# RMSNorm on one core: the first eight rows loaded as four transfers over interleaved partitions

## Chip, core and metric

The kernel runs on one core of a Trainium2 chip. The metric is the device time of one execution in microseconds, taken as the median over runs.

## What is computed

Every row of 512 numbers is divided by its root mean square and multiplied by `gamma`; there are 16 x 1024 = 16,384 rows in float32.

```
def reference(x, gamma):          # x: 16 x 1024 x 512, gamma: 512
    eps = 1e-5
    rms = np.sqrt(np.mean(x ** 2, axis=-1, keepdims=True) + eps)
    return (x / rms * gamma).astype(np.float32)
```

Input and output have 33.55 MB each, and there is little arithmetic per byte.

## The kernel before

The 16,384 rows are cut into four tiles of 128 partitions x 32 rows; a partition's 32 rows of a tile lie side by side in memory (64 KB). Three buffers in SBUF, `slots[0]` to `slots[2]`, hold one whole tile each; tile 3 uses slot 0 again. Each tile is worked on in groups of rows, nine groups in all: tile 0 as rows 0 to 6, 7 to 15 and 16 to 31, the other tiles in halves of 16 rows.

For a group, ScalarE (ACT) squares the rows (L96), VectorE (DVE) sums the squares (L97), ACT takes the root (L102) and DVE the reciprocal (L103). Then the rows are shared out. GpSimd (POOL) takes the last `share` rows and multiplies them by the reciprocal (L109) and by `gamma_b` (L110). The other rows are scaled by ACT, one instruction a row (L118), and multiplied by gamma by DVE in one instruction (L122), which reads gamma from PSUM. Gamma gets to all partitions by a matmul of a column of ones with `gamma_row` (L66); ACT copies it to `gamma_b` (L165) for POOL.

The order of the instructions is written out by hand (`manual_schedule`). All transfers are issued by SyncE (SP), by the helpers `load` (L45) and `store` (L49); SP works through them in the order of the program. At the start the order is: row 0 of tile 0, rows 1 to 7, gamma in five pieces (L58), rows 8 to 15, rows 16 to 31, and half of tile 1:

```
    load(0, 0, 0, 1)
    load(0, 0, 1, 8)
    for c0, c1 in zip(pieces, pieces[1:]):
        nc.sync.dma_start(out=gamma_row[:, c0:c1], in_=gamma.unsqueeze(0)[:, c0:c1])
    load(0, 0, 8, 16)
    load(0, 0, 16, 32)
    load(1, 1, 0, 16)
```

The semaphores of the transfers go round in a ring of eight: the ninth transfer waits until the first has landed, the tenth for the second, and so on. In the trace, the ninth, `load(0, 0, 16, 32)`, waits on the semaphore of the first, and the tenth, `load(1, 1, 0, 16)`, on that of the second.

All further loads and stores are listed in `transfers`, called once per group after DVE's multiplication. The list `before_scale` holds the transfers and POOL instructions that touched the rows of a slot; `times_gamma` uses it to tell the scheduler which earlier accesses need no wait of DVE's own.

Of the kernel before, what the change touches and what calls it, by code (L numbers as in the profile page):

```python
# [9 lines left out]
def kernel(  # L10
# [6 lines left out]
    nc = tc.nc  # L17
# [8 lines left out]
    N, D = xf.shape  # L26
# [3 lines left out]
    xv = xf.rearrange("(t p r) d -> t p r d", p=P, r=R)  # L30
# [9 lines left out]
    slots = [const.tile([P, R, D], fp32, name=f"slot{i}") for i in range(3)]  # L40

    before_scale = []

    def load(t, slot, r0, r1):
        dma = nc.sync.dma_start(out=slots[slot][:, r0:r1], in_=xv[t][:, r0:r1])  # L45
        before_scale.append((slot, r0, r1, dma))
# [3 lines left out]
        before_scale.append((slot, r0, r1, dma))  # L50

    gamma_row = const.tile([1, D], fp32)
    pieces = (0, 128, 224, 320, 416, D)

    load(0, 0, 0, 1)
    load(0, 0, 1, 8)
    for c0, c1 in zip(pieces, pieces[1:]):
        nc.sync.dma_start(out=gamma_row[:, c0:c1], in_=gamma.unsqueeze(0)[:, c0:c1])  # L58
    load(0, 0, 8, 16)
# [106 lines left out]
    for k, group in enumerate(groups):  # L166
        t, g, n, pieces, share = group
# [45 lines left out]
```

## Time and profile before

| | |
|---|---|
| median of 3 runs | 161.58 us (161.57 to 161.68) |
| span of the profiled execution, the time it gives for itself | 160.2 us |
| DVE busy | 112.0 us (70%) |
| ACT busy | 107.8 us (67%) |
| POOL busy | 106.4 us (66%) |
| PE busy | 2.0 us (1%) |
| moved by DMA | 67.12 MB, mean 419 GB/s over the span |
| first instruction of DVE's last multiplication (L122) | 132.05 us, 7.09 us long |

The span is the time from the first to the last instruction of the program; the runs are timed around it and are 1.4 us longer. Busy times of different engines overlap. In the lines below, L45 means line 45 of the kernel file; `A <- B` after a count names what an engine waited for; "slot<-in_x_dram" is a transfer from the input to a slot. A window's line gives its limits in us, its length, the busy time of PE, PE's weight loads, DVE, ACT and POOL with the number of instructions in brackets, the granted TensorE clock, the mean busy share of the 16 DMA engines, and the rate in GB/s.

### The profile page before, as it was taken

How to read it: one execution, taken by the hardware profiler on the slowest of the kernel's cores; microseconds unless marked ns; L12 is line 12 of the kernel's file. 1: busy time of each engine (PE TensorE's matmuls, PEld its weight loads, DVE VectorE, ACT ScalarE, POOL GpSimd, SP SyncE). 2: the span in 40 equal slices, each digit the busy share in tenths (PEclk: the TensorE clock that was granted, in tenths of full speed). 3: DMA queues.
4: the chain of work that ended last, by engine and by line, in shares of the span. 5: the costliest groups of instructions: out<-in, count | busy, mean ns of one | idle time of the engine just before them, and what ended most of it. 6: DMA issues, size and time to landing. Idle time of an engine off the chain costs nothing.

```text
span 160.2 us, 276 instructions
## 1 busy us (share of the span) xinstructions
PE 2.0 (1%) x2; PEld 0.5 (0%) x2; DVE 112.0 (70%) x39; ACT 107.8 (67%) x108; POOL 106.4 (66%) x24
## 2 busy tenths in 40 slices
PE   0050000000000000000000000000000000000000
PEld 0010000000000000000000000000000000000000
DVE  0018098899798999999999999999999009700000
ACT  3071967976999998999899899989960990000000
POOL 1000951994999599999999999999999980000000
DMA  5999999899999899999999999996996996999994
GB/s 189 431 421 475 442 401 458 340 446 491 417 435 494 388 379 383 426 450 475 434 401 426 483 401 393 524 491 295 524 491 295 524 491 295 401 491 417 401 450 196
DMA packets 2747, 67.12 MB, mean 419 GB/s; under 512 B 313, under 2 KB 314, under 8 KB 826
## 3 DMA queue, kind: packets, MB, share of 16 engines
q1 hardware_dynamic: 2746, 67.11, 98.1%
q14 instruction: 1, 0.01, 0.0%
HBM read 33.56 MB, written 33.55 MB: 419 GB/s over the span
## 4 chain that ended last, share of the span: by engine, by line
DVE 59%; ACT 22%; DMA 4%; ACTq 0%; issue 0%; SPq 0%
DVE ss L97 36%; DVE slot L122 23%; ACT slot L118 8%; ACT slot L96 7%; ACT sq_psum L96 6%; DMA slot<-in_x_dram 4%; DVE ss L103 1%; ACT ss L102 1%; ACTq L208 0%; ACT gamma_b L165 0%; SPq L45 0%; ACTq L96 0%
## 5 line engine op out<-in xcount | busy, mean ns | idle before, releaser
L109 POOL TENSOR_TENSOR slot<-slot,ss 128x3584 f32<-128x3584 f32 (+2 forms) x9 | 47.0, 5218 | 24.1 <-DVE ss L103 24.1
L110 POOL TENSOR_TENSOR slot<-slot,gamma_b 128x3584 f32<-128x3584 f32 (+2 forms) x9 | 59.3, 6587 | 0.7
L97 DVE TENSOR_REDUCE ss<-sq_psum 128x7 f32<-128x3584 f32 (+1 forms) x13 | 42.2, 3247 | 13.7 <-ACT sq_psum L96 13.7
L118 ACT ACTIVATE slot<-slot,ss 128x512 f32<-128x512 f32 x75 | 47.3, 706 | 4.7 <-DVE ss L103 4.7
L122 DVE TENSOR_TENSOR slot<-slot,gamma_psum 128x4608 f32<-128x4608 f32 (+2 forms) x9 | 41.3, 4590 | 8.7 <-ACT slot L118 8.7
L96 ACT ACTIVATE sq_psum<-slot 128x3584 f32<-128x3584 f32 (+1 forms) x13 | 34.6, 2658 | 6.4 <-DMA slot<-in_x_dram 5.7
L97 DVE TENSOR_REDUCE ss<-slot 128x9 f32<-128x4608 f32 x3 | 14.9, 4954 | 4.4 <-ACT slot L96 4.2
L97 DVE TENSOR_REDUCE ss<-sq_sbuf 128x5 f32<-128x2560 f32 x5 | 14.0, 2803 | 0.0
L96 ACT ACTIVATE slot<-slot 128x4608 f32<-128x4608 f32 x3 | 12.1, 4033 | 0.0
L96 ACT ACTIVATE sq_sbuf<-slot 128x2560 f32<-128x2560 f32 x5 | 11.6, 2321 | 0.0
L102 ACT ACTIVATE ss<-ss,eps_t 128x16 f32<-128x16 f32 (+2 forms) x9 | 2.7, 305 | 11.9 <-DVE ss L97 11.9
L103 DVE RECIPROCAL ss<-ss 128x16 f32<-128x16 f32 (+2 forms) x9 | 2.1, 236 | 0.4 <-ACT ss L102 0.4
L66 PE MATMUL gamma_psum<-gamma_row,ones_col 1*128 1x512 f32 x2 | 2.0, 1122 | 8.6 <-DMA gamma_row<-in_gamma_dram 8.6
L72 ACT ACT_TABLE_LOAD x1 | 1.3, 1283 | 1.2 <-PEq L197 1.2
L165 ACT COPY gamma_b<-gamma_psum 128x512 f32<-128x512 f32 x1 | 0.6, 567 | 0.0
L66 PEld LDWEIGHTS gamma_psum<-gamma_row,ones_col 1*128 1x128 f32 x2 | 0.5, 308 | 8.6 <-issue 8.6
L64 POOL MEMSET ones_col<- 1x128 f32 x1 | 0.2, 195 | 0.3 <-POOLq L197 0.3
L197 POOL MEMSET const-float32-0.0<- 128x1 f32 x1 | 0.1, 99 | 0.2 <-issue 0.2
L72 ACT ACTIVATE table<-eps_t 128x1 f32<-128x1 f32 x1 | 0.2, 202 | 0.0
L197 POOL MEMSET const-bfloat16-1.0<- 128x1 bf16 x1 | 0.1, 102 | 0.0
L197 POOL MEMSET const-uint8-127<- 128x1 uint8 x1 | 0.1, 102 | 0.0
L197 POOL MEMSET const-float32-1.0<- 128x1 f32 x1 | 0.1, 99 | 0.0
(1 smaller groups left out, 0.1 us busy)
## 6 DMA issues: line engine op xcount, KB each, us to landing
slot<-in_x_dram SPq DMA_DIRECT2D x5, 4096.0 KB, 21.9
out_dram<-slot SPq DMA_DIRECT2D x3, 4096.0 KB, 23.4
slot<-in_x_dram SPq DMA_DIRECT2D x1, 5888.0 KB
out_dram<-slot SPq DMA_DIRECT2D x1, 3328.0 KB, 21.8
slot<-in_x_dram SPq DMA_DIRECT2D x1, 2304.0 KB, 14.3
slot<-in_x_dram SPq DMA_DIRECT2D x1, 2048.0 KB, 9.9
slot<-in_x_dram SPq DMA_DIRECT2D x1, 1792.0 KB, 7.0
out_dram<-slot SPq DMA_DIRECT2D x3, 256.0 KB
```

Source lines behind the costliest of these rows:

```text
L66: nc.tensor.matmul(gamma_psum[:, 0], ones_col, gamma_row, start=True, stop=True)
L72: nc.scalar.activation(out=table, in_=eps_t, func=AF.Sqrt)
L96: nc.scalar.activation(out=sq[:, :m], in_=rows, func=AF.Square)
L97: nc.vector.tensor_reduce(out=ss[:, r : r + m, 0], in_=sq[:, :m], axis=mybir.AxisListType.X, op=OP.add)
L102: nc.scalar.activation(out=ss[:, :n, 0], in_=ss[:, :n, 0], func=AF.Sqrt, bias=eps_t, scale=1.0 / D)
L103: nc.vector.reciprocal(out=ss[:, :n, 0], in_=ss[:, :n, 0])
L109: nc.gpsimd.tensor_tensor(out=part, in0=part, in1=by_row, op=OP.mult)
L110: last = nc.gpsimd.tensor_tensor(out=part, in0=part, in1=gamma_b.to_broadcast([P, share, D]), op=OP.mult)
L118: nc.scalar.activation(out=x[:, g + r, :], in_=x[:, g + r, :], func=AF.Copy, scale=rstd[:, r])
L122: scaled = nc.vector.tensor_tensor(out=part, in0=part, in1=gamma_psum.to_broadcast([P, r1 - r0, D]), op=OP.mult)
L165: nc.scalar.copy(out=gamma_b[:, 0], in_=gamma_psum[:, 0])
L197: nc = _bacc.Bacc("TRN2", target_bir_lowering=False, num_devices=1)
```

## The change

Rows 0 to 7 of tile 0 were two transfers over all 128 partitions, one of row 0 (2 KB a partition) and one of rows 1 to 7 (14 KB a partition). They become four transfers that each carry all eight rows (16 KB a partition) for part of the partitions: 0, 8, 16, ... (16 partitions), then 4, 12, 20, ... (16), then 2, 6, 10, ... (32), then 1, 3, 5, ... (64). Gamma's five pieces of 128, 96, 96, 96 and 96 numbers become three of 192, 160 and 160. The number of transfers ahead of `load(0, 0, 16, 32)` stays eight.

```
-    pieces = (0, 128, 224, 320, 416, D)
-
-    load(0, 0, 0, 1)
-    load(0, 0, 1, 8)
+    pieces = (0, 192, 352, D)
+
+    for p0, step in ((0, 8), (4, 8), (2, 4), (1, 2)):
+        dma = nc.sync.dma_start(out=slots[0][p0::step, 0:8], in_=xv[0][p0::step, 0:8])
+        before_scale.append((0, 0, 8, dma))
     for c0, c1 in zip(pieces, pieces[1:]):
         nc.sync.dma_start(out=gamma_row[:, c0:c1], in_=gamma.unsqueeze(0)[:, c0:c1])
     load(0, 0, 8, 16)
```

## The prediction

> **What bounds the kernel now.** I read the page's slices first, then busy time by stage, then the order of time around the change, then the waits of the transfer queue. The slices:
>
> ```profile
> span 160.2 us, 276 instructions
> ...
> DVE  0018098899798999999999999999999009700000
> ...
> DMA  5999999899999899999999999996996996999994
> ...
> DMA packets 2747, 67.12 MB, mean 419 GB/s; under 512 B 313, under 2 KB 314, under 8 KB 826
> ```
>
> No compute engine is busy in the last fifth of the span, but the DMA digits are at 9 nearly throughout, and 67.12 MB at 419 GB/s is the whole span. The same by stage (columns: length of the window, busy time of each engine, then clock, DMA share, GB/s):
>
> ```profile
> 0.00:1.70 1.70, 0.00 (x0) 0.00 (x0) 0.00 (x0) 0.55 (x1) 0.44 (x6) 1.00 0.00 0
> 1.70:2.20 0.50, 0.00 (x0) 0.00 (x0) 0.00 (x0) 0.50 (x1) 0.00 (x0) 1.00 0.75 86
> 2.20:2.70 0.50, 0.00 (x0) 0.00 (x0) 0.00 (x0) 0.44 (x2) 0.00 (x0) 1.00 0.85 307
> 2.70:5.20 2.50, 0.00 (x0) 0.00 (x0) 0.00 (x0) 0.00 (x0) 0.00 (x0) 1.00 1.05 419
> 5.20:7.70 2.50, 0.00 (x0) 0.00 (x0) 0.00 (x0) 0.00 (x0) 0.00 (x0) 1.00 1.03 430
> ...
> 34.00:139.00 105.00, 0.00 (x0) 0.00 (x0) 95.17 (x33) 87.20 (x93) 93.41 (x15) 1.00 1.00 430
> 139.00:158.00 19.00, 0.00 (x0) 0.00 (x0) 0.14 (x1) 0.00 (x0) 0.00 (x0) 1.00 1.00 433
> ```
>
> From 2.7 us to 158 us the 16 DMA engines never have a free moment. What can move the end is only the start-up before 2.7 us, the cost of the packets, or an empty queue. The chain of waits names DVE L97 and L122, which is misleading here: that chain ends at 139.14 us with L122, and 20 us of transfers follow.
>
> The order of time at the start, and the queue's waits:
>
> ```profile
> 0.74 0.86 SPq L45 DMA_DIRECT2D slot<-in_x_dram  x2
> 1.65 1.48 SPq L58 DMA_DIRECT2D gamma_row<-in_gamma_dram  x5
> 3.17 5.39 SPq L45 DMA_DIRECT2D slot<-in_x_dram  x3
> 8.31 3.16 ACT L96 ACTIVATE sq_psum<-slot 128x3584 f32<-128x3584 f32 x1 [5.66 <-DMA slot<-in_x_dram]
> ...
> 27.35 0.35 SPq L49 DMA_DIRECT2D out_dram<-slot  x1
> ```
>
> ```profile
> SPq L49 <- DVE slot L122: 56.1, 5, 26.0
> ...
> SPq L45 <- DMA slot<-in_x_dram: 4.2, 1, 4.2
> ```
>
> SP issues everything. Eight transfers go out by 3.5 us, the ninth and tenth wait for the first and second to land (the 4.2 us), and then SP sits until the first store at 27.35.
>
> **The packets of the first rows.** The trace's DMA packet records give: 2 KB 84 ns, 14 KB 535 ns, 16 KB 611 ns, 32 KB 1213 ns, 64 KB 2418 ns (medians). From 32 KB to 64 KB that is 27.2 B/ns on one engine, the same for loads and stores; 16 engines make 435 GB/s, and the windows show 430 to 433. So every engine runs at its own fixed rate all the time. The engines' first packets begin between 1.75 and 2.54 us (mean 2.02). The early ones took 468, 581 and 544 ns instead of 84, so some 0.4 us is a first read's latency. The 16 engines end the eight rows between 7.21 and 7.90 us, mean 7.49.
>
> **The change, part by part.**
> Bytes are equal: eight rows are 16 KB per partition, 2.10 MB, eight 16 KB packets per engine, 8 x 611 = 4.89 us. Before it was 8 x 84 + 8 x 535 = 4.95 us. Gain 0.06 us.
>
> Start-up: before, 7.49 us at the mean end minus 1.75 (first packet) minus 4.89 leaves 0.85 us lost. A read's latency of 0.4 us (468 or so less 84) stays, so at most 0.45 us can be won, the 0.06 included. With 16 descriptors of 16 KB instead of 128 of 2 KB for the first transfer, all engines should get their first packet almost together; I take 0.35, near the upper end, because most of the loss is the spread of first starts. The bound below is zero, if the slow packets (14 KB ones took up to 820 ns) come from the memory and not from the spread.
>
> Issue: two issues become four, five gamma pieces three; still eight before the ninth, so the waits on the first and second transfer keep their places (now on 16-partition transfers, landing earlier). SP's time: 4 x 0.44 + 3 x 0.29 = 2.6 us against 2.43 (0.74 to 3.17), so `load(0, 0, 8, 16)` goes out some 0.2 us later. A packet starts 1.0 us after its issue (0.74 to 1.75), so it is there at 4.4; the engines need it at about 7.2. Cost nothing, 2.8 us of cover. The subset transfers follow each other by 0.44 us, while one 16 KB packet lasts 0.61: no engine runs out. Without cover, each late issue would cost 0.44 us.
>
> Gamma: the records show five pieces on one engine, 22 or 27 ns each and 9 for the semaphore, 0.16 us; three make 0.1. That engine was the first to end the eight rows (7.21 us), so this is worth nothing. The matmul still starts behind the landing near 8.6 us and `gamma_b` is needed at 15.63: 5 us of cover.
>
> L96 now waits for four transfers instead of two. Nothing on ACT is queued behind it that could run earlier; DVE's first L97 and POOL's first L109 wait with it. Any shift X of these rows moves the first store from 27.35 by X. Loads queued before it are 12.58 MB, 29.3 us at 429 GB/s after an effective start of 2.6, so the queue runs dry at 31.9; a store needs 1.0 us from issue, leaving 3.5 us, and a later landing pushes both ends alike. Later covers are larger: the last store is issued at 139.2 while earlier ones occupy the engines to about 149. So compute costs nothing in all cases, and DMA time lost or won at the start arrives at the end one for one.
>
> Where the packets go is the open term. [...] In the new transfers 16 engines write partitions eight, four or two apart. If the 27.2 B/ns is the engine's own limit, the extra is 0. If it is the limit of the place written, and two engines meet at one place, each 611 ns packet takes 1222: 8 x 0.611 = 4.89 us more. Engines that start apart collide less: two of the 16 first starts differ by 0.3 us on average, saved once in each of four transfers, 1.2 us. That leaves 3.7 us, and minus the 0.35 won at the start +3.3.
>
> I take +3.3, because the gain is capped at 0.45 and the packet rows are so constant (16 KB: 611 ns in all 128 cases) that I read a fixed limit on each engine's own path to its place, with no reserve for a second engine, as a little likelier than a limit inside the engine. Both ends stay in the range.
>
> [...]
>
> **The rivals.**
> *Engine limit (faster):* no place is shared. For it: nothing in the trace shows a shared limit. Time 161.58 - 0.35 = 161.23; it decides if the first eight rows are in by 7.4 us.
> *Nothing arrives:* the spread of starts comes back through the first read of each new transfer (first 14 KB packets of 722 and 736 ns instead of 535: about 0.2 us over three added boundaries shared between engines, or 0.1 to 0.3), and eats the gain: 161.5.
> *The transfers aren't what they say:* a stepped partition pattern could be cut into 2 KB runs. 64 x 84 = 5.38 us instead of 4.95, +0.43: 162.0. Against it: rows r to r+8 of a partition lie side by side on both ends, as in the third load of the program, whose packets are of 16 KB.
>
> **How the numbers follow.** The span, 160.2, is 1.4 us below the median of the runs, 161.58; I add differences to the median. Shared places 0.52 at 161.58 + 3.3 = 164.9 (its own range 162.8 to 166.5: from 2 x 0.611 us more, if only the first two transfers collide, to all eight packets doubled); small loss as in the 2 KB case 0.08; nothing arrives 0.15; engine limit 0.25. A measurement can tell about 0.2%, 0.32 us. So faster 0.25, same 0.15, slower 0.60. The range must take in both signs: 161.1 (a gain of 0.45) to 166.5 (4.89 lost).
>
> **What would show it.** Shared places: the GB/s of the windows 2.70:5.20 and 5.20:7.70 fall to 220 to 300, L96 starts near 11.6 instead of 8.31, the first store is issued near 30.7, the last near 142.5, and the 16 KB packets of the start take 0.9 to 1.2 us. Engine limit: 430 GB/s already from 2.2 us on, L96 near 7.9, everything after it earlier by the same. Wrong in any case: a DMA share below 0.95 after 10 us (the queue ran dry), or a change in the end that differs from the change in L96's start.

## The result, and the profile after

The changed kernel takes 164.25 us (median of 6 runs, 163.24 to 164.40) against 161.63 for the kernel before (161.44 to 162.61): 1.014 times as long, interval 1.0117 to 1.0164. That interval is 1.9 to 2.7 us more; the forecast was 3.3, with a range that began at a small gain. The profiled execution took 164.4 us, 162.6 of it span, 2.4 more than before.

The slices of the page, after. Behind the loop over the subsets every line of the file has a number one higher than before: the squares are L97, DVE's product L123; the subsets are issued by L56.

```profile
span 162.6 us, 277 instructions
...
DVE  0006349799798999999999999999999009700000
...
DMA  5999999999999989999999999999899899799991
...
DMA packets 2647, 67.12 MB, mean 413 GB/s; under 512 B 339, under 2 KB 342, under 8 KB 726
```

The same bytes, DMA at 9 as before, and compute again silent in the last fifth: the bound has not changed. The same windows as before show where the rate fell (last column, GB/s). A packet counts, with all its time and bytes, in the window in which it starts, so a share in a short window can be above 1.

```profile
1.70:2.20 0.50, 0.00 (x0) 0.00 (x0) 0.00 (x0) 0.50 (x1) 0.00 (x0) 1.00 0.67 180
2.20:2.70 0.50, 0.00 (x0) 0.00 (x0) 0.00 (x0) 0.44 (x2) 0.00 (x0) 1.00 1.25 360
2.70:5.20 2.50, 0.00 (x0) 0.00 (x0) 0.00 (x0) 0.00 (x0) 0.00 (x0) 1.00 0.92 249
5.20:7.70 2.50, 0.00 (x0) 0.00 (x0) 0.00 (x0) 0.00 (x0) 0.00 (x0) 1.00 1.02 354
7.70:12.00 4.30, 1.75 (x2) 0.50 (x2) 0.00 (x0) 1.49 (x1) 0.00 (x0) 1.00 0.97 404
...
34.00:139.00 105.00, 0.00 (x0) 0.00 (x0) 95.09 (x34) 89.39 (x96) 95.50 (x16) 1.00 1.01 435
```

The share stays above 0.9 while the rate drops from 419 to 249 and from 430 to 354: the engines are busy all the time, but a packet takes longer (in order of time, the first three sixteens of 16 KB packets have medians of 0.94 to 1.04 us, against 0.611 for 16 KB before). From 9 us on the rate is back. In the order of time the first square and the first store both come 2.20 us later, and the end 2.4:

```profile
0.73 2.48 SPq L56 DMA_DIRECT2D slot<-in_x_dram  x4
3.26 1.02 SPq L59 DMA_DIRECT2D gamma_row<-in_gamma_dram  x3
4.32 1.85 SPq L45 DMA_DIRECT2D slot<-in_x_dram  x3
...
10.51 3.16 ACT L97 ACTIVATE sq_psum<-slot 128x3584 f32<-128x3584 f32 x1 [7.86 <-DMA slot<-in_x_dram]
...
29.55 0.35 SPq L49 DMA_DIRECT2D out_dram<-slot  x1
```

From the packet records of both traces I worked out the time lost up to a moment, as the moment less the bytes moved by then at 429 GB/s, a mean over the 16 engines:

| up to | 2.5 us | 5 us | 9 us | 18 us |
|---|---|---|---|---|
| before | 2.32 | 2.50 | 2.60 | 2.53 |
| after | 2.35 | 3.33 | 4.12 | 4.09 |

So compared with before nothing more is lost up to 2.5 us, 0.8 more between 2.5 and 5 us, 0.7 more between 5 and 9 us, and nothing more up to 18 us. That makes 1.5 us. The rest is unevenness: the engine that finishes last ends 0.46 us after the mean of the 16 engines' last packets before (158.99 and 158.53) and 1.39 us after it now (161.43 and 160.04). 1.5 and 0.9 make the 2.4. Most of the unevenness is there early: when the engines begin their first 32 KB packet, behind the first sixteen rows, the last of them is 1.0 us behind their mean (14.93 us), against 0.4 before (12.76 us). All engines move about the same 4.19 MB, and the lag stays to the end. (The records don't name the engine; a packet is taken to follow the one that ended as it began.)

### The profile page after: what moved, and what is told of

The parts are those of the page before. It is cut to its first block, busy times and chain, and to the rows that moved or that the text cites. A ratio compares the mean times of both kernels' runs of the same rounds, so it can differ in the third digit from the quotient of the medians.

```text
span 162.6 us, 277 instructions
## 1 busy us (share of the span) xinstructions
PE 2.0 (1%) x2; PEld 0.5 (0%) x2; DVE 112.0 (69%) x39; ACT 107.8 (66%) x108; POOL 106.4 (65%) x24
## 4 chain that ended last, share of the span: by engine, by line
DVE 58%; ACT 22%; DMA 5%; SPq 1%; ACTq 0%; issue 0%
DVE ss L98 35%; DVE slot L123 22%; ACT slot L119 8%; ACT slot L97 7%; ACT sq_psum L97 6%; DMA slot<-in_x_dram 5%; SPq L56 1%; DVE ss L104 1%; ACT ss L103 1%; ACTq L209 0%; ACT gamma_b L166 0%; ACTq L97 0%
## 5 line engine op out<-in xcount | busy, mean ns | idle before, releaser
L123 DVE TENSOR_TENSOR slot<-slot,gamma_psum 128x4608 f32<-128x4608 f32 (+2 forms) x9 | 41.3, 4588 | 8.7 <-ACT slot L119 8.7
L97 ACT ACTIVATE sq_psum<-slot 128x3584 f32<-128x3584 f32 (+1 forms) x13 | 34.6, 2659 | 8.6 <-DMA slot<-in_x_dram 7.9
L97 ACT ACTIVATE slot<-slot 128x4608 f32<-128x4608 f32 x3 | 12.1, 4031 | 0.0
L97 ACT ACTIVATE sq_sbuf<-slot 128x2560 f32<-128x2560 f32 x5 | 11.6, 2321 | 0.0
```

Source lines behind the costliest of these rows:

```text
L97: nc.scalar.activation(out=sq[:, :m], in_=rows, func=AF.Square)
L123: scaled = nc.vector.tensor_tensor(out=part, in0=part, in1=gamma_psum.to_broadcast([P, r1 - r0, D]), op=OP.mult)
```

## The experiments

Theory A: two or more engines write into the same place of SBUF and share its rate. Theory B: the source rows, 512 KB apart, disturb one another in the memory. Theory C: four transfers pay for four starts. The first three edits replace the loop over the four subsets in the changed kernel. Every kernel is timed beside the kernel before on the same chip, which took 161.5 us (medians 161.46 to 161.54).

### Is it the number of transfers, the source or the destination?

**Four transfers without subsets**

```
-    for p0, step in ((0, 8), (4, 8), (2, 4), (1, 2)):
-        ...
+    for r in (0, 2, 4, 6):
+        load(0, 0, r, r + 2)
```

> Eight rows in four transfers of two rows each over all 128 partitions, gamma in three pieces: the number of transfers of the change without its subsets of partitions. Theory A (two engines share a place in SBUF when the partitions are a subset) and theory B (the memory side: rows 512 KB apart are read at the same time) both expect the time of before, 161.6 us, within 0.4. Theory C (four transfers instead of two cost their own start each) expects the changed kernel's 164.2.

Measured: 161.64 us, ratio 0.9999 (0.9974 to 1.0024). The four starts and the three gamma pieces cost no time that shows at the end, so C falls as the cause of the slowdown. They do cost something at the start: the first square comes at 8.68 us, 0.37 later than before, and by 9 us the engines have lost 3.00 us on average against 2.60 before. Some 0.14 of these 0.4 us are the 4 KB packets (32 x 159 ns make 5.09 us against 4.95 for the eight rows before). The rest may be part of the change's loss as well; that isn't separated here.

**Neighbouring partitions**

```
+    for p0, p1 in ((0, 16), (16, 32), (32, 64), (64, 128)):
+        dma = nc.sync.dma_start(out=slots[0][p0:p1, 0:8], in_=xv[0][p0:p1, 0:8])
```

> Four transfers of 16, 16, 32 and 64 partitions as in the change, but of neighbouring partitions (0-15, 16-31, 32-63, 64-127), so that the rows read together are 64 KB apart. [...] Theory B: the source is nearly one piece, so 161.4 to 162.2. Theory C: as the change, 164.2.

Measured: 167.33 us, 1.0352 (1.0335 to 1.0369), far above B's and C's. Of the three only A allows such a time; how much slower it makes these transfers, no run before had shown. Its windows:

```profile
2.70:5.20 2.50, 0.00 (x0) 0.00 (x0) 0.00 (x0) 0.00 (x0) 0.00 (x0) 1.00 1.10 138
5.20:8.20 3.00, 0.00 (x0) 0.00 (x0) 0.00 (x0) 0.00 (x0) 0.00 (x0) 1.00 0.83 153
8.20:13.00 4.80, 0.00 (x0) 0.00 (x0) 0.00 (x0) 0.00 (x0) 0.00 (x0) 1.00 1.01 212
13.00:18.00 5.00, 2.04 (x2) 0.50 (x2) 0.12 (x1) 3.16 (x1) 0.00 (x0) 1.00 0.96 374
```

The rate comes in steps, and the packet records, in order of time, have the same steps: a 16 KB packet takes 2.01 us in partitions 16 to 31, then 1.6 to 2.2 for each engine's first in partitions 32 to 63, and 1.14 to 1.42 from there to partition 127, where 128 partitions in one transfer need 0.611.

**Destination as in the change, source near**

```
+    for p0, step, s0, s1 in ((0, 8, 0, 16), (4, 8, 16, 32), (2, 4, 32, 64), (1, 2, 64, 128)):
+        dma = nc.sync.dma_start(out=slots[0][p0::step, 0:8], in_=xv[0][s0:s1, 0:8])
```

> Destination as in the change (every eighth, fourth, second partition), but the source rows are those of 16, 16, 32 and 64 neighbouring partitions, so the first eight rows of tile 0 are exchanged between partitions; nothing else is changed. Theory A: as the change, 164.2 us within 0.5. Theory B: 161.4 to 162.2. Theory C: 164.2, so it stands against theory B only.

Measured: 164.26 us, 1.0151 (1.0114 to 1.0187), as the change. B falls; what counts is which partitions a transfer writes.

### How hard is a collision, and does spread help?

To see a steady rate I loaded rows 16 to 31 of tile 0 in subsets, in the kernel before, in the middle of a full queue.

```
-    load(0, 0, 16, 32)
+    for p0, p1 in ((0, 64), (64, 128)):
+        dma = nc.sync.dma_start(out=slots[0][p0:p1, 16:32], in_=xv[0][p0:p1, 16:32])
+        before_scale.append((0, 16, 32, dma))
```

> The kernel before, with rows 16 to 31 of tile 0 (4.19 MB, 9.8 us at the rate of 128 partitions) loaded as two transfers over partitions 0-63 and 64-127; the transfer queue stays full. Theory A (a place is a fixed group of partitions, and two engines share one throughout each half): about half rate, 210 to 230 GB/s between 13 and 31 us, and 161.6 + 9.8 = 171.4 us within 0.8. Rival (only the start of the kernel is sensitive, when the engines start together): within 0.5 of 161.6.

```
+    for p0 in (0, 1, 2, 3, 4, 5, 6, 7):
+        dma = nc.sync.dma_start(out=slots[0][p0::8, 16:32], in_=xv[0][p0::8, 16:32])
```

> The kernel before, with rows 16 to 31 of tile 0 loaded as eight transfers over every eighth partition, starting at 0, 1, 2, 3, 4, 5, 6, 7 in this order. [...] Rival (the step of the partitions itself is what costs, not the places): the same time as with the order 0, 4, 1, 5, 2, 6, 3, 7, within 0.5.

The same eight transfers in turn, in the order 0, 4, 1, 5, 2, 6, 3, 7:

```
+    for p0 in (0, 4, 1, 5, 2, 6, 3, 7):
```

> [...]

The window from 15 to 30 us, for the kernel before, the halves, the grouped order and the order in turn, one line each:

```profile
15.00:30.00 15.00, 0.00 (x0) 0.00 (x0) 9.32 (x6) 12.00 (x10) 8.67 (x3) 1.00 1.00 426
```
```profile
15.00:30.00 15.00, 0.00 (x0) 0.00 (x0) 7.83 (x5) 7.47 (x8) 8.69 (x3) 1.00 1.01 210
```
```profile
15.00:30.00 15.00, 0.00 (x0) 0.00 (x0) 7.77 (x5) 7.46 (x8) 8.76 (x3) 1.00 1.01 210
```
```profile
15.00:30.00 15.00, 0.00 (x0) 0.00 (x0) 7.84 (x5) 7.46 (x8) 8.68 (x3) 1.00 1.00 221
```

| | time, us | ratio to before | 32 KB packet, us |
|---|---|---|---|
| partitions 0-63, 64-127 | 172.08 | 1.0647 (1.0631 to 1.0663) | 2.56 |
| every eighth, grouped | 171.79 | 1.0634 (1.0617 to 1.065) | 2.54 |
| every eighth, in turn | 170.74 | 1.0566 (1.0546 to 1.0587) | 2.35 |
| all 128 (before) | 161.52 | | 1.21 |

The DMA share stays at 1.00 to 1.01 while the packets take 1.94 to 2.1 times as long: by theory A that is two engines in one place, each at about half its rate; the records show the packet times and not the places. The rival of the first run (only the start is sensitive) falls. In the run of halves the sixteen packets just behind the halves go to all 128 partitions and still take 1.5 to 2.2 us, and the sixteen after them take 1.21 again, as if the records lagged there by about one packet. In turn, packets are 7% shorter and the run 1.05 us faster, so the order matters and not the step alone; but the relief is small, and the rate stays near the half, at 221 GB/s against 426. Which engines work side by side, and on which partitions, the records don't show.

### Was it the late first packet?

```
+    load(0, 0, 0, 1)
+    for p0, step in ((0, 8), (4, 8), (2, 4), (1, 2)):
+        dma = nc.sync.dma_start(out=slots[0][p0::step, 1:8], in_=xv[0][p0::step, 1:8])
```

> Row 0 first over all 128 partitions as before, then rows 1 to 7 in the four subsets of the change, gamma in two pieces (eight transfers ahead of the ninth). If the first packet came late in the change (2.10 us against 1.75) because its first issue steps through the partitions, the first packet is back at 1.75 us and 0.3 us of the loss is gone: 163.7 to 164.1 us. If it came late because it carried few descriptors or long ones, it would also be back, and the sharing alone stays: the time alone does not tell these apart, the run with neighbouring partitions does.

Measured: 164.23 us, 1.0153 (1.0131 to 1.0175). The first packet is back at 1.74 us, and the time is that of the change. My expectation of 0.3 us of time was a miss, within the scatter of these runs. The records show where it went: by 9 us the mean loss is 3.85 us against 4.12 in the change, the 0.3 expected, but the last engine ends 1.9 us behind the mean instead of 1.4.

### Which of the four transfers collide?

```
-    load(0, 0, 16, 32)
+    for p0 in (0, 1):
+        dma = nc.sync.dma_start(out=slots[0][p0::2, 16:32], in_=xv[0][p0::2, 16:32])
```

> The kernel before, with rows 16 to 31 of tile 0 loaded as two transfers, even and odd partitions. [...] Reading A1 (an engine gets four neighbours of the list, 16 engines start on half of the places): 2.35 to 2.55 us a 32 KB packet and 168 to 171.5 us. Reading A2 (with 64 or 32 partitions in steps the engines are spread over all places as with 128): 1.21 us a packet and 161.4 to 162.0.

```
+    for p0 in (0, 1, 2, 3):
+        dma = nc.sync.dma_start(out=slots[0][p0::4, 16:32], in_=xv[0][p0::4, 16:32])
```

> As the run with even and odd partitions, but four transfers of every fourth partition (32 each). A1: two packets an engine and transfer, half of the places at a time, 168 to 171.5 us. A2: 161.4 to 162.0.

The same window, even and odd first, then the fourths:

```profile
15.00:30.00 15.00, 0.00 (x0) 0.00 (x0) 9.32 (x6) 12.15 (x10) 8.81 (x3) 1.00 0.99 422
```
```profile
15.00:30.00 15.00, 0.00 (x0) 0.00 (x0) 9.32 (x6) 12.18 (x10) 8.84 (x3) 1.00 0.99 424
```

Full rate, and 1.213 us for each packet of this transfer, from the first on: reading A2, in so far as nothing collides. Which engine gets which partition the records don't say. The times are 161.84 for the fourths (1.0026, 1.0004 to 1.0047) and 162.36 for even and odd (1.0073, 1.0029 to 1.0116; single runs from 161.5 to 163.9). The second is above A2's range, while its profiled span, 159.8 us, is shorter than that of before; what lengthens some of its runs is open.

So of the four transfers of the change only the two sixteens should collide. Without them:

```
-    pieces = (0, 192, 352, D)
+    pieces = (0, 128, 256, 384, D)
-    for p0, step in ((0, 8), (4, 8), (2, 4), (1, 2)):
+    for p0, step in ((0, 4), (2, 4), (1, 2)):
```

> The change with its two transfers of 16 partitions made into one of 32 (every fourth partition from 0), then 32 from 2 and 64 from 1 as in the change; gamma in four pieces, so that eight transfers stand ahead of the ninth. A2 (only the sixteens collide): 161.4 to 162.1 us, the first square near 8.4 us. A1 (all four collide at first and then drift apart): 163.5 to 164.4, the first square near 10.3.

Measured: 162.71 us, 1.0068 (1.0055 to 1.0082), between the two readings; the first square starts at 9.45 us. More than half of the extra time is gone, and the rest stands in another place:

```profile
2.70:5.20 2.50, 0.00 (x0) 0.00 (x0) 0.00 (x0) 0.00 (x0) 0.00 (x0) 1.00 0.92 347
5.20:8.20 3.00, 0.00 (x0) 0.00 (x0) 0.00 (x0) 0.00 (x0) 0.00 (x0) 1.00 0.92 328
```

The window up to 5.2 us has risen from 249 to 347 GB/s, but the next one stays at 328 (350 for the change in the same window). In the records nearly every engine moves its second to fourth packet at 0.61 us each, and then most have one of 0.8 to 1.8 us in the transfer of 64. The mean lost time by 9 us is 3.66 us, against 4.12 for the change and 2.60 before, so only 0.5 of the 1.5 us is gone by this measure. A larger part of the gain is evenness: the last engine ends 0.6 us behind the mean instead of 1.4. The last experiment takes that transfer without the short ones ahead:

```
+    pieces = (0, 128, 224, 320, 416, D)
+    for p0, step in ((0, 2), (1, 2)):
```

> The eight rows as two transfers of 64 partitions, even and odd, gamma in five pieces as before. No sixteens, so nothing collides. Open is the second loss of the run without the sixteens (162.7 us; the trace loses 0.9 us between 5 and 9 us, in packets of its transfer of 64 partitions that take 1.0 to 2.0 us). Reading B1 (a stepped transfer of 64 partitions in 16 KB pieces loses this by itself, early in the kernel): 162.3 to 162.9 and again below 360 GB/s between 5.2 and 8.2 us. Reading B2 (it takes the row of short transfers ahead of it): 161.3 to 161.8 and 420 to 440 GB/s there.

Measured: 161.81 us, 1.0018 (1.0005 to 1.003), the upper edge of B2's range, with 427 GB/s in the window that B2 names:

```profile
2.70:5.20 2.50, 0.00 (x0) 0.00 (x0) 0.00 (x0) 0.00 (x0) 0.00 (x0) 1.00 0.96 400
5.20:8.20 3.00, 0.00 (x0) 0.00 (x0) 0.00 (x0) 0.01 (x1) 0.00 (x0) 1.00 1.00 427
```

The transfer of 64 does not lose this by itself; the second loss came only with the shorter stepped transfers before it. Why is open. That the fifth to tenth issues fall into the same microseconds (3.12 to 6.69 us) is not enough: with four transfers of two rows they went out from 2.86 to 5.98 us, and only 0.1 us was lost between 5 and 9 us.

### Is there a better start?

```
-    load(0, 0, 0, 1)
-    load(0, 0, 1, 8)
+    load(0, 0, 0, 8)
```

> One transfer of eight rows over all 128 partitions, gamma in six pieces so that eight transfers still stand ahead of the ninth. By the packet rows it saves 8 x 84 + 8 x 535 against 8 x 611, 0.06 us; the second transfer no longer has a start of its own, 0.1 to 0.2 us. All theories: 161.3 to 161.7.

Measured: 161.48 us, 0.9995 (0.9986 to 1.0005): as expected, and no gain that can be told from none. The first square moves to 7.95 us.

## Why the prediction was right, and where it was not

**The bound, and what costs nothing: right.** DMA rate sets the end (435 GB/s from 34 to 139 us), compute has slack everywhere (DVE's last product ends at 141.3 us of 162.6), and the queue never ran dry (a DMA share of 0.92 to 1.02 in the stages from 2.7 to 158 us). The first store moved with the first square, 2.20 us each. The end moved by 2.4, nearly one for one. The sum was made with the engines' mean, but the slowest of the 16 engines counts, which is 0.9 us of it.

**The collision: right in kind, much too large, and near in size by luck.** The term was 8 packets x 0.611 = 4.89 us, less 1.2 for spread, so 3.7 us. That two engines meet at one place, in all four transfers or in the first two alone, no row of the kernel before shows, and no run shows the places; what the runs showed instead is the packet's duration. First, not eight packets collide. In the middle of the queue, 32 and 64 partitions in steps run at 1.213 us a 32 KB packet, as 128 do; of the subsets in the change only the sixteens run at half rate (2.35 to 2.54 us a packet). Their two packets would make 1.22 us, the figure that the prediction had as the low end of this case. The table of lost time has 0.8 by 5 us, and taking the sixteens out brought 1.54 us of time (164.25 to 162.71), about half of it by evenness. In order of time, the first four sixteens of packets in the change have medians of 0.94, 0.98, 1.04 and 0.62 us; with one transfer of eight rows they have 1.10, 0.61, 0.61 and 0.61. The first packet is slow in any case, and the second and third carry the collision of the first two, if the records lag here as they seem to behind the halves. Second, a quarter of the collision saved by spread would leave about 2.1 us a packet in a steady stream; the two orders had 2.54 and 2.35.

In the place of what is missing stand two things that the prediction did not have: 0.7 us lost between 5 and 9 us, whose cause is open, and the 0.9 us of unevenness. Together they are 1.6 of the 2.4 us. So the direction and the kind of the loss were foreseen, and the size came out near because a term that was 2.5 us or more too large was partly made up for by two that were left out. The window from 2.7 us was forecast at 220 to 300 GB/s and showed 249; the next one was forecast the same and showed 354, which fits later transfers that do not collide. The first square came at 10.51 us, not near 11.6.

**The start: wrong.** I took 0.35 us of gain; it was nothing. The first packet came later, not earlier (2.10 us against 1.75), and the first issue, with a step, takes 0.59 us against 0.38 for all partitions. That is 0.2 of the 0.35 us; the rest is not explained. With 16 neighbours the first issue took 0.39 us and the first packet came at 1.75, so it is the step and not the small number. The issues of the subsets (shortest, median and longest in ns), with a step and for neighbours:

```profile
L56 SPq DMA_DIRECT2D slot<-in_x_dram x4: 568/585/594, 0.7 to 2.6; - x4
```
```profile
L56 SPq DMA_DIRECT2D slot<-in_x_dram x4: 392/409/526, 0.7 to 2.1; - x4
```

The engines then start closer together (first packets from 2.10 to 2.60 us, against 1.75 to 2.54 before), and the two effects cancel by 2.5 us (2.35 us lost against 2.32). SP's row of issues was mis-sized because each issue took 0.59 us and not 0.44: `load(0, 0, 8, 16)` went out at 4.32 us, not near 3.4; the packets it brings are needed only behind 8.5 us, so the cover held.

**Gamma: right.** The matmul follows its landing to 10.25 us, `gamma_b` is copied at 17.84, and three pieces in the run with four whole-width transfers cost nothing.

**The rivals.** Engine limit falls with the half rate of the 64-partition halves (210 GB/s against 426), in which all engines stay busy (share 1.01). "Nothing arrives" falls by its size. The cut into 2 KB runs falls too: the records of the change show 16 KB packets.

## What to carry to other kernels

Where DMA sets the time, ask of a transfer over part of the partitions which ones it writes, and not only how many bytes or packets it has: here two transfers of 64 partitions ran at 210 GB/s as halves (0 to 63, 64 to 127) and at 422 as even and odd ones. The sign was a busy share near 1 (1.01) with a falling GB/s, and the packet's duration showed it (2.56 us against 1.21). A transfer in the middle of a full queue shows the steady rate of an odd pattern better than one at the start, where the engines' first packets were slow anyway (a median of 1.10 us against 0.61 with one transfer of eight rows). When a rate term spans several transfers, bound it transfer by transfer; here the steady runs put it on two of four. And look at the slowest engine as well as the mean: here a lag of 1.0 us at the start stayed, 1.4 us at the end.

## What the runs showed of the hardware

- 16 neighbouring partitions (16 to 31): 2.01 us for a 16 KB packet; 64 neighbours 1.14 to 1.29; 128 partitions 0.611. Sixteen at every eighth: 2.35 to 2.54 us for 32 KB against 1.213 for 128 partitions.
- 32 partitions at every fourth, or 64 at every second, run at 422 to 424 GB/s between 15 and 30 us, where 128 partitions have 426.
- As the first transfer of the kernel, one whose partitions have a step takes SP 0.54 to 0.61 us to issue, whether it has 16, 32 or 64 partitions, against 0.38 to 0.39 without a step, and its first packet comes 0.3 to 0.4 us later (2.06 to 2.14 us against 1.73 to 1.75).
